# A chunk's transposed key and its scores in one bank, another order of the first LayerNorm, and shorter intervals in the scaling of token rows

## The chip, the cores and the metric

The kernel runs on one core of a Trainium2 chip. The metric is the device time of one execution in microseconds (us). The core has five engines with queues of their own, which work at once and wait for each other through semaphores: TensorE (PE in the profile, with its weight loads as PEld), VectorE (DVE), ScalarE (ACT), GpSimd (POOL) and SyncE (SP), whose queue issues most DMA transfers. PE writes its products to PSUM, eight banks of 512 float32 columns on 128 partitions; ACT and DVE read them from there.

## What is computed

One decoder block over 1,024 tokens behind 16 learned meta tokens, so 1,040 positions, each of width 1,024. The change touches three places of it: the LayerNorm that comes first, the mLSTM mixer, and the `alpha * h` that the second LayerNorm adds.

```python
h = LN(concat(meta, x))                       # the first LayerNorm
p = h @ w_in + b_in                           # -> u_s5 | q | k | v | o | i | f | g_s5 | g_m
y_s5 = GLU(GELU(S5(u_s5)))
y_m  = (o * HeadNorm(mLSTM(q, k, v, i, f))) @ m_w_out
h = LN(alpha * h + (sigmoid(g_s5) * y_s5 + sigmoid(g_m) * y_m) @ w_o)
h = LN(alpha * h + relu(h @ w_up + b_up)**2 @ w_down)
...
# mLSTM, four heads, chunk by chunk with a running state (c, n):
s = einsum("bhsd,bhjd->bhsj", q_c, k_c) * w_intra       # scores
num = s @ v_c + w_inter * (q_c @ c_st)
den = sum(s) + w_inter * (q_c . n_st)
c_new = decay * c_st + sum_j w_k[j] * outer(k_c[j], v_c[j])
```

## The kernel before

Products that need more than one pass over the array are made from a high and a low part of each factor (`whi`, `wlo`, `hT_hi`, `hT_lo`): three matmuls (L235 to L237, `mm3`) for each product. A job is a block of columns of the combined projection; it loads raw weights (`wraw`), ACT rounds them to `whi` (L221), DVE takes the rest as `wlo` (L222), and PE runs through the jobs in the order of a list. Beside the jobs there are lanes: generators (mLSTM, convolution, S5, the scaling of token rows) that yield an interval after each step. `mm3` advances a clock after every second of its terms by an estimate of the time that they take on PE, and each lane whose next step has come due by that clock issues it there (`pump`). A scheduler then settles each engine's order; only weight splits are raised in priority.

PSUM is handed out in two rings: five banks with the tag `mm` and three with the tag `sd` (`sdps`). Dependencies are kept by bank: two engines that use one bank, even other columns of it, follow one another.

**The first LayerNorm** (`ln0_pipe`, L1278 to L1447) is laid out by hand, as the list of tokens `LN0_PROG` (L66 to L76). Rows come in nine tiles `x0` to `x8` of 128 positions (the last of 16), in the groups 0, 1, 2-3, 4-5 and 6-8. The tokens are:

- `sT0 sT1` are DVE's statistics of tile T (L1291, two halves), `gT` their sum (L1296), `qG` ACT's square root for a group (L1300), `cG0` to `cG3` four small DVE steps to its inverse (L1306 to L1312), `bT` the shift that ACT needs (L1317).
- `nTa`, `nTd`, `nTl`, `nTh` normalise tile T, on ACT (L1328), on DVE (L1330), or on DVE by halves (L1326). `TT` transposes it on PE (L1343) into four banks that two tiles share, two blocks of 128 rows of width in each (`ln`), or, for the first two tiles, four blocks in each.
- `uTK`, `vPK`, `zK` copy block K out of a bank, scaled and shifted (`hf`), by ACT (L1360, suffix `a`) or DVE (L1362, suffix `d`). `HPJ` rounds half J of the pair P to `hT_hi` (ACT, L1381) and sends `hf` to DRAM, `LPJ` takes the rest as `hT_lo` (DVE, L1379).
- `WI` and `lI` split the weights of job I (L221, L222). `FIT` is job I over tile T in plain float32 (L1398). `AIB`, `BIB`, `CIB` are its three passes over block B of 256 positions (L1390: `whi` by `hT_hi`, `whi` by `hT_lo`, `wlo` by `hT_hi`), and `EIB` is ACT's copy of the sum (L298).

The order of the tokens is, but for the scheduler's shifts, the order on each engine. PE needs the four `sd` and `mm` banks of a pair emptied before it can transpose the next pair into them.

**mLSTM** (L440 to L536), for each of four heads over nine chunks, issues `A(c+1)` and then `B(c)`. `A` transposes the chunk's key (L466, tile `pk`), which ACT scales into `kw` (L468), and multiplies key by query (L471, tile `pS`), which DVE weighs into `sw` (L473). `B` makes the output `pn` from the state `C` and from `sw` (L481, L482) and the update `pu` from `kw` (L485); DVE folds it into `C` (L490), ACT and DVE read `pn` (L499 to L503). Each of the four tiles is a bank of the ring of three. Four chunks on, `N` normalises them, and PE transposes the outcome `hraw` (L523).

**The scaling of token rows** (`ah_scale`, L1454 to L1474) starts with the last job of the projection. It loads eight tiles of rows, multiplies and adds on DVE (L1471), waiting the interval `AHY` (3.6) after each of the sixteen steps, and stores them.

Of the kernel before, what the change touches and what calls it, by code (L numbers as in the profile page):

```python
# [12 lines left out]
AF = mybir.ActivationFunctionType  # L13
OP = mybir.AluOpType
P = 128
# [7 lines left out]
DK = 128  # L23
DV = 256
NCH = 9
# [29 lines left out]
Y5 = [3.2, 1.86, 2.37, 2.47]  # L55
AFT = 0
AH_START = "run7"
AHY = 3.6
UPY = 1.0
PRY = 1.07  # L60
TBY = 1.47
# [2 lines left out]
VAFT = 2  # L64
LOAD0 = "x0 x1 w0 c0 x2 w1 c1 x3 x4 w2 x5 w3 x6"
LN0_PROG = " ".join((  # L66
# [9 lines left out]
LN0_GROUPS = ((0,), (1,), (2, 3), (4, 5), (6, 7, 8))  # L76
BLK = ((0, 256), (256, 640), (640, 1040))
# [10 lines left out]
def chunk(c):  # L88
    return (0, META) if c == 0 else (META + (c - 1) * P, P)
# [32 lines left out]
def decoder_block(  # L122
# [5 lines left out]
    v_, a_, g_, t_ = nc.vector, nc.scalar, nc.gpsimd, nc.tensor  # L128
# [9 lines left out]
    def slot(name, dt=F32):  # L138
        return big.tile([P, SLOT], dt, tag="s", name=name)
# [4 lines left out]
    def sdps(name="sd"):  # L144
        return psum.tile([P, 512], F32, tag="sd", bufs=3, name=name)
# [17 lines left out]
    ident = const.tile([P, P], F32, name="ident")  # L163
# [276 lines left out]
    def mlstm(h):  # L440
        while (h, 1) not in QK:
            yield 0.5
        qT, kT, vt = QK[h, 0], QK[h, 1], VT[h]
        gB, wiB = slot("gB"), slot("wiB")
# [5 lines left out]
        for c in range(NCH):  # L450
            c0, n = chunk(c)
# [8 lines left out]
        kws, sws, Cs = {}, {}, {}  # L460

        def A(c):
            c0, n = chunk(c)
            if c < NCH - 1:
                ps = sdps("pk")
                t_.transpose(ps[:n, :DK], kT[:, c0:c0 + n], ident)  # L466
                kws[c] = mid.tile([P, DK], F32, tag="kw", bufs=2, name="kw")
                a_.activation(kws[c][:n], ps[:n, :DK], AF.Copy, scale=gB[:n, c0 + n - 1:c0 + n])  # L468
            if c > 0:
                ps = sdps("pS")  # L470
                t_.matmul(ps[:, :P], kT[:, c0:c0 + n], qT[:, c0:c0 + n], start=True, stop=True)  # L471
                sws[c] = mid.tile([P, P], F32, tag="sw", bufs=2, name="sw")
                v_.tensor_tensor(sws[c], ps[:, :P], gB[:, c0:c0 + n], op=OP.mult)  # L473

# [30 lines left out]
        def N(half, hm):  # L505
# [12 lines left out]
            for f in range(2):  # L518
# [7 lines left out]
                yield 1.2  # L526

        A(0)
        yield 1.5
        for c in range(NCH):  # L530
            if c + 1 < NCH:
                A(c + 1)
            yield ML[h]
            B(c)
            yield ML[h]
            if c == 5:  # L536
                yield from N(0, nrm[0])
# [916 lines left out]
    def ah_scale():  # L1454
# [4 lines left out]
        for t in range(9):  # L1459
# [10 lines left out]
            for i, op in enumerate((OP.mult, OP.add)):  # L1470
                v_.tensor_tensor(r[:, :D], r[:, :D], gb[i][:, :D], op=op)  # L1471
                yield AHY
            nc.sync.dma_start(ah_dr[(t - 1) * P:t * P, :], r[:, :D])
# [31 lines left out]
    for w in ORDER.split():  # L1505
        n, i = w[0], int(w[1:])
# [669 lines left out]
```

## Time and profile before

| | before |
|---|---|
| median of 3 runs | 1524.61 us (1524.44 to 1526.71) |
| the profiled execution | 1524.99 us, of which the span from the first to the last instruction is 1523.2 us |
| mean granted clock of TensorE | 0.995 |
| DVE busy | 1049.4 us, 69% of the span |
| ACT busy | 667.9 us, 44% |
| DMA, mean rate over the span | 173 GB/s |
| the scaling's 16 steps on DVE (L1471) | 638.1 to 709.8 us of the span, 1.22 us each |

The profile is of one execution. Times in its views count from the first instruction. A row of the view of time gives the start, the length of the group, the engine, the line, the operation with output and inputs, how many, and in brackets how long the engine stood idle before it and for whom. Matmuls overlap, so that two starts, not one length, give what a matmul takes on PE. In the view of stretches the columns are the stretch, its length, PE's busy time with the number of instructions, the granted clock as a share of the full one, and DMA. In the view of waits they are who waited for whom, the sum, how often, and the longest.

The first LayerNorm fills the span up to 76.6 us, where the first job for the value projection starts (L348). Head 0 of mLSTM starts at 138.9 us and the last head's last key is transposed at 521.6 us.

### The profile page before, as it was taken

Reading aid. Unit: us, or ns where it says so; the run is one execution under the profiler, and the core shown is the slowest. Engines: PE = TensorE matmul, PEld = TensorE weight load, DVE = VectorE, ACT = ScalarE, POOL = GpSimd, SP = SyncE. Lnnn points to the kernel's source line nnn. Section 1 sums busy time; section 2 is a strip of 40 time slices with the busy share of each in tenths; the row PEclk is TensorE's granted clock in tenths of the full one; section 3 lists DMA queues with packets and bytes.
Section 4 is the critical chain, followed back from the end, with each engine's and each line's share of the span. In section 5 each row is a group of like instructions: output and inputs, shape, how many; then the busy total and the mean of one; then the engine's idle time right before and its main releaser. Section 6 shows DMA issues by size and latency. Waiting matters only on the chain.

```text
span 1523.2 us, 20345 instructions
## 1 busy us (share of the span) xinstructions
PE 1498.7 (98%) x7581; PEld 1268.1 (83%) x7581; DVE 1049.4 (69%) x1901; ACT 667.9 (44%) x1033; POOL 81.8 (5%) x183
## 2 busy tenths in 40 slices
PE   7999899999999999999999999999999999999997
PEld 7998799988998888887888888888888888888886
DVE  7776755675675356788797575766666579867786
ACT  5641634454565533345443253444444524333330
POOL 0000000033330000000000001000000000000000
PEclk9999999999999999999999999999999999999999
DMA  8513332256754238876352248644443799667543
GB/s 303 192 46 91 82 98 87 70 156 155 183 136 125 69 126 331 297 264 211 111 193 69 97 128 268 187 153 149 145 147 128 251 374 343 211 236 246 196 166 111
DMA packets 123635, 264.06 MB, mean 173 GB/s; under 512 B 14648, under 2 KB 36864, under 8 KB 123536
## 3 DMA queue, kind: packets, MB, share of 16 engines
q1 hardware_dynamic: 112064, 233.79, 45.1%
q0 software_dynamic: 11472, 28.97, 7.7%
q8 instruction: 60, 0.98, 0.3%
q14 instruction: 39, 0.32, 0.1%
HBM read 191.67 MB, written 86.64 MB: 183 GB/s over the span
## 4 chain that ended last, share of the span: by engine, by line
PE 74%; issue 17%; DMA 4%; DVE 3%; ACT 1%; SPq 0%; POOLq 0%; ACTq 0%; DVEq 0%
PE mm L237 19%; PE mm L235 19%; PE mm L236 19%; PE sd L236 3%; PE sd L235 3%; PE sd L237 3%; PE mm L1390 2%; DMA wdr<-in_wdn_dram 1%; DMA x<-in_x_dram 1%; PE pn L481 1%; PE pn L482 1%; PE pu L485 1%; DMA da<-act_dr 1%; DMA wiB<-wrow_dr 1%; PE pS L471 1%
## 5 line engine op out<-in xcount | busy, mean ns | idle before, releaser
L235 PE MATMUL mm<-hT_hi,whi 128*128 128x512 f32 (+3 forms) x600 | 228.7, 381 | 1.7 <-ACT whi L1068 1.7
L237 PE MATMUL mm<-hT_hi,wlo 128*128 128x512 f32 (+3 forms) x600 | 223.9, 376 | 0.6 <-DVE wlo L1069 0.6
L236 PE MATMUL mm<-hT_lo,whi 128*128 128x512 f32 (+3 forms) x600 | 224.1, 374 | 0.0
L235 PEld LDWEIGHTS mm<-hT_hi,whi 128*128 128x128 f32 x600 | 112.9, 188 | 19.9 <-ACT whi L1068 2.2
L237 PEld LDWEIGHTS mm<-hT_hi,wlo 128*128 128x128 f32 x600 | 112.9, 188 | 19.7 <-DVE wlo L1069 1.6
L236 PEld LDWEIGHTS mm<-hT_lo,whi 128*128 128x128 f32 x600 | 113.0, 188 | 16.3
L1875 ACT ACTIVATE dwh<-wdr 128x1024 fp32r<-128x1024 f32 x56 | 58.9, 1053 | 107.0 <-DVE wdr L1860 39.2
L237 PE MATMUL sd<-dwh,dal 128*128 128x512 f32 x240 | 94.4, 393 | 0.0
L236 PE MATMUL sd<-dwl,dah 128*128 128x512 f32 x240 | 94.3, 393 | 0.0
L235 PE MATMUL sd<-dwh,dah 128*128 128x512 f32 x240 | 92.0, 393 | 0.0
L1872 DVE TENSOR_TENSOR dal<-da,dah 128x1024 fp32r<-128x1024 f32 x56 | 68.2, 1219 | 25.7 <-ACT dah L1871 9.7
L236 PE MATMUL mm<-dwl,dah 128*128 128x512 f32 (+1 forms) x224 | 84.7, 378 | 0.1
L237 PE MATMUL mm<-dwh,dal 128*128 128x512 f32 (+1 forms) x224 | 84.6, 378 | 0.0
L235 PE MATMUL mm<-dwh,dah 128*128 128x512 f32 (+1 forms) x224 | 83.3, 377 | 0.0
L1871 ACT ACTIVATE dah<-da 128x1024 fp32r<-128x1024 f32 x56 | 58.8, 1052 | 53.2 <-DMA da<-act_dr 32.3
L222 DVE TENSOR_TENSOR wlo<-wraw,whi 128x1024 fp32r<-128x1024 f32 (+1 forms) x44 | 53.6, 1221 | 34.0 <-ACT whi L221 32.9
L1876 DVE TENSOR_TENSOR dwl<-wdr,dwh 128x1024 fp32r<-128x1024 f32 x56 | 68.3, 1220 | 9.6 <-ACT dwh L1875 9.0
L235 PE MATMUL mm<-whi,hT_hi 128*128 128x256 f32 (+1 forms) x256 | 73.9, 289 | 0.0
L237 PE MATMUL mm<-whi,hT_lo 128*128 128x256 f32 (+1 forms) x256 | 72.7, 284 | 0.0
L236 PE MATMUL mm<-wlo,hT_hi 128*128 128x256 f32 (+1 forms) x256 | 72.6, 284 | 0.0
L237 PE MATMUL mm<-th,wul 128*128 128x512 f32 x156 | 61.5, 394 | 0.0
L236 PE MATMUL mm<-tl,wuh 128*128 128x512 f32 x156 | 61.4, 394 | 0.0
(481 smaller groups left out, 3669.9 us busy)
## 6 DMA issues: line engine op xcount, KB each, us to landing
da<-act_dr SPq DMA_DIRECT2D x56, 512.0 KB, 5.7
wdr<-in_wdn_dram SPq DMA_DIRECT2D x56, 512.0 KB, 6.5
wur<-in_wup_dram SPq DMA_DIRECT2D x32, 512.0 KB, 4.9
act_dr<-upy SPq DMA_DIRECT2D x64, 256.0 KB, 2.8
wraw<-in_wf_dram SPq DMA_DIRECT2D x28, 512.0 KB, 5.9
wu_dr<-wpre SPq DMA_DIRECT2D x21, 512.0 KB, 6.0
wpre<-wu_dr POOLq DMA_DIRECT2D x21, 512.0 KB, 5.4
wraw<-ws_dr SPq DMA_DIRECT2D x32, 256.0 KB, 3.5
```

Source lines behind the costliest of these rows:

```text
L222: todo.append(lambda e=v_, r=r, hi=hi, lo=lo, n=n: e.tensor_tensor(lo[:, :n], r[:, :n], f32(hi[:, :n]), op=OP.subtract))
L235: t_.matmul(ps, ah, bh, start=(i == 0 and part[0]), stop=False, skip_group_check=skip)
L236: t_.matmul(ps, ah, bl, start=False, stop=False, skip_group_check=skip)
L237: t_.matmul(ps, al, bh, start=False, stop=(i == n - 1 and part[1]), skip_group_check=skip)
L471: t_.matmul(ps[:, :P], kT[:, c0:c0 + n], qT[:, c0:c0 + n], start=True, stop=True)
L481: t_.matmul(pn[:, :257], qi[:, c0:c0 + n], Cs[c][:, :257], start=True, stop=False)
L482: t_.matmul(pn[:, :257], sws[c], vt[c][:, :257], start=False, stop=True)
L1390: t_.matmul(acc[w][:, :c1 - c0], jobs[i].w[0][a][:, k * P:(k + 1) * P], (hT_hi, hT_lo)[b][:, k, c0:c1], start=(first and k == 0), stop=(la ...
L1871: a_.activation(ah[:, :D], a[:, :D], AF.Copy)
L1872: v_.tensor_tensor(alo[:, :D], a[:, :D], f32(ah[:, :D]), op=OP.subtract)
L1875: a_.activation(wh, raw[i], AF.Copy)
L1876: v_.tensor_tensor(wl, raw[i], f32(wh), op=OP.subtract)
```

## The change

First, `A(c)` takes one bank `pkS` where it took two: the transposed key goes to columns 128 to 255, the scores to columns 0 to 127. PE does both one behind the other, then ACT reads the key, then DVE the scores. Second, `LN0_PROG` is rewritten: the copies of a bank go to one engine, where they alternated between two; the splits `W0` and `W1` stand earlier, and so do the statistics of tiles 4 and 5 and `n4d`; `L20`, `L21` and the statistics of tile 7 stand behind one another later. Third, `AHY` is 2.8 instead of 3.6.

```diff
-AHY = 3.6
+AHY = 2.8
...
-    "X30 s00 s01 g0 q0 s10 c00 c01 c02 c03 n0l n0h s11 g1 T0l T0h u00a u01a q1 u02d u03a c10 c11 c12 c13 n1d",
-    "u04a u05a u06d u07a F00 s20 s21 F10 T1 u10a u11d u12a u13d u14a u15d u16a u17d F20 g2 s30 s31 g3 W0 H00",
-    "F01 q2 H01 c20 c21 c22 c23 b2 b3 F11 n2a n3a E00 L00 L01 F21 E10 W1 s40 s41 g4 T2 l1 W2 E20 s50 s51 g5 q3",
-    "T3 l0 W3 c30 c31 c32 F30 v11a v13d v12a c33 n4d v17a v16a v10d F31 b5 H10 v14d v15d n5a l3 L10 T4 H11 s70",
-    "T5 E30 L11 A01 v26a v22a v20d B01 v21d v23d C01 v25d H20 v24d A11 v27d E01 B11 L20 H21 C11 L21 A02 E11",
-    "s71 B02 l2 C02 g7 s60 A22 E02 s61 g6 B22 s80 s81 C22 g8 q4 A31 E22 c40 c41 c42 c43 B31 b8 b7 b6 n8a C31",
-    "n7a A12 n6a B12 E31 C12 T8 E12 T7 z83a z82d z86a z84d z80a z85d z81a T6 z87a H8 L8 A32 v33a v30d v31a",
-    "v37d B32 v34a v36d v35a v32d C32 H31 A21 E32 L31 H30 B21 L30 C21 A03 E21 B03 C03 A33 E03 B33 C33 A13 E33",
+    "X30 s00 s01 g0 q0 s10 c00 c01 c02 c03 n0l n0h s11 g1 T0l T0h u00a q1 u01a u02a u03a u04d u05d c10 c11",
+    "u06d u07d c12 c13 n1d W0 F00 s20 s21 W1 F10 g2 s30 s31 T1 g3 u10a u11a u12a u13a q2 u14d u15d u16d u17d",
+    "F20 H00 c20 c21 c22 c23 b2 b3 H01 F01 n2a s40 s41 g4 n3a F11 s50 s51 g5 q3 E00 L00 F21 E10 c30 c31 c32",
+    "c33 b5 T2 n4d L01 E20 n5a T3 W2 l1 F30 v10a v11a v12a v13a v14d v15d v16d v17d F31 H10 l0 W3 H11 T4 L10",
+    "T5 E30 L11 s60 s61 A01 B01 C01 v20a v21a v22a v23a v24d v25d v26d v27d E01 H20 g6 A11 l2 B11 H21 s70 s71",
+    "C11 L20 E11 g7 A02 L21 B02 s80 s81 C02 g8 q4 E02 A22 l3 B22 c40 c41 c42 c43 C22 b8 b7 b6 E22 A31 n8a B31",
+    "n7a C31 n6a A12 E31 B12 C12 T8 E12 T7 z80d z81d z82d z83d z84d z85d z86d z87d T6 H8 L8 A32 v30a v31a v32a",
+    "v33a v34d v35d v36d v37d B32 C32 H31 H30 A21 E32 L31 B21 L30 C21 A03 E21 B03 C03 A33 E03 B33 C33 A13 E33",
...
         def A(c):
             c0, n = chunk(c)
+            ps = sdps("pkS")
             if c < NCH - 1:
-                ps = sdps("pk")
-                t_.transpose(ps[:n, :DK], kT[:, c0:c0 + n], ident)
+                t_.transpose(ps[:n, P:P + DK], kT[:, c0:c0 + n], ident)
+            if c > 0:
+                t_.matmul(ps[:, :P], kT[:, c0:c0 + n], qT[:, c0:c0 + n], start=True, stop=True)
+            if c < NCH - 1:
                 kws[c] = mid.tile([P, DK], F32, tag="kw", bufs=2, name="kw")
-                a_.activation(kws[c][:n], ps[:n, :DK], AF.Copy, scale=gB[:n, c0 + n - 1:c0 + n])
+                a_.activation(kws[c][:n], ps[:n, P:P + DK], AF.Copy, scale=gB[:n, c0 + n - 1:c0 + n])
             if c > 0:
-                ps = sdps("pS")
-                t_.matmul(ps[:, :P], kT[:, c0:c0 + n], qT[:, c0:c0 + n], start=True, stop=True)
                 sws[c] = mid.tile([P, P], F32, tag="sw", bufs=2, name="sw")
                 v_.tensor_tensor(sws[c], ps[:, :P], gB[:, c0:c0 + n], op=OP.mult)
```

Behind `A`, every line of the new program stands one lower than in the old one.

On DVE, in the first LayerNorm, the inverse root of the group of tiles 4 and 5 (`y_147`) and the normalisation of tile 4 (`n4d`, the row with `x_120`) stood in the old program behind `L00`, `L01` and the splits `l1` and `l0`, with small steps of S5 and a copy (L1362) between them:

```order
L1306 RECIPROCAL y_147<-y_147 128x2
L572 SCALAR_TENSOR_TENSOR s_t_1210<-s_t_1209,s_t_1210 128x16
L1308 SCALAR_TENSOR_TENSOR u_152<-mv_142,y_147 128x2
L573 TENSOR_SCALAR s_dt<-s_t_1210 128x16
L577 TENSOR_SCALAR s_t_1209<-s_t_1209 128x16
L1310 SCALAR_TENSOR_TENSOR u_152<-u_152,y_147 128x2
L1362 TENSOR_SCALAR hf<-ln_335,ln0t 128x256
L575 SCALAR_TENSOR_TENSOR s_dt<-s_dt,s_t_1210 128x16
L578 CAST s_ni<-s_t_1209 128x16
L1312 SCALAR_TENSOR_TENSOR y_147<-u_152,y_147 128x2
L575 SCALAR_TENSOR_TENSOR s_dt<-s_dt,s_t_1210 128x16
L1330 TENSOR_SCALAR x_120<-x_120,mv_142,y_147 128x1024
```

In the new one they stand ahead of the splits (L222) and ahead of the copies of the pair of tiles 2 and 3:

```order
L1307 RECIPROCAL y_147<-y_147 128x2
L1309 SCALAR_TENSOR_TENSOR u_152<-mv_142,y_147 128x2
L1311 SCALAR_TENSOR_TENSOR u_152<-u_152,y_147 128x2
L568 TENSOR_SCALAR s_t_1210<-s_lam 128x16
L1313 SCALAR_TENSOR_TENSOR y_147<-u_152,y_147 128x2
L569 TENSOR_SCALAR s_t_1209<-s_t_1210 128x16
L1318 SCALAR_TENSOR_TENSOR u_152<-mv_142,y_147 128x1
L1331 TENSOR_SCALAR x_120<-x_120,mv_142,y_147 128x1024
L1380 TENSOR_TENSOR hT_lo<-hf,hT_hi 128x4x256
L297 MEMSET cpre 128x3
L570 TENSOR_SCALAR s_t_1209<-s_t_1209 128x16
L222 TENSOR_TENSOR wlo<-wraw,whi 128x1024
```

So the normalisation of tile 4 has passed `L01` (the row L1380), two splits and the copy.

Further down on DVE, the low parts of the pair of tiles 4 and 5 (`L20`, `L21`) followed the copies of that pair almost at once, in the old program:

```order
L1362 TENSOR_SCALAR hf<-ln_408,ln0t 128x256 x2
L575 SCALAR_TENSOR_TENSOR s_dt<-s_dt,s_t_1210 128x16
L1362 TENSOR_SCALAR hf<-ln_409,ln0t 128x256
L1362 TENSOR_SCALAR hf<-ln_410,ln0t 128x256 x2
L1362 TENSOR_SCALAR hf<-ln_411,ln0t 128x256
L576 TENSOR_SCALAR s_dt<-s_dt 128x16
L1379 TENSOR_TENSOR hT_lo<-hf,hT_hi 128x4x256
L579 TENSOR_TENSOR s_dt<-s_dt,s_ni 128x16
L1379 TENSOR_TENSOR hT_lo<-hf,hT_hi 128x4x256
L1291 BN_STATS st_424<-x_133 128x6
L222 TENSOR_TENSOR wlo<-wraw,whi 128x1024
```

In the new one there are statistics of tiles 6 and 7 (`x_128`, `x_133`) and a split ahead of each or between them:

```order
L1292 BN_STATS st_435<-x_128 128x6 x2
L1363 TENSOR_SCALAR hf<-ln_410,ln0t 128x256 x2
L1363 TENSOR_SCALAR hf<-ln_411,ln0t 128x256 x2
L573 SCALAR_TENSOR_TENSOR s_t_1210<-s_t_1209,s_t_1210 128x16
L1297 BN_AGGR mv_143<-st_435 128x2
L222 TENSOR_TENSOR wlo<-wraw,whi 128x1024
L1292 BN_STATS st_495<-x_133 128x6 x2
L1380 TENSOR_TENSOR hT_lo<-hf,hT_hi 128x4x256
L574 TENSOR_SCALAR s_dt<-s_t_1210 128x16
L578 TENSOR_SCALAR s_t_1209<-s_t_1209 128x16
L1297 BN_AGGR mv_143<-st_495 128x2
L1380 TENSOR_TENSOR hT_lo<-hf,hT_hi 128x4x256
```

DVE has two copies fewer there (four of the pair's eight, where it had six), and two statistics and a split more ahead of `L20`.

On PE, in head 0 of mLSTM, one chunk's transposed key and scores were parted by a matmul of the job that runs beside them:

```order
L485 MATMUL pu<-v_881,kw 128x257
L466 MATMUL pk<-ident,kT 128x128
L237 MATMUL mm<-hT_hi,wlo 128x512
L471 MATMUL pS<-qT,kT 128x128
L235 MATMUL mm<-hT_hi,whi 128x512
```

In the new program they stand together:

```order
L486 MATMUL pu<-v_881,kw 128x257
L466 MATMUL pkS<-ident,kT 128x128
L468 MATMUL pkS<-qT,kT 128x128
L237 MATMUL mm<-hT_hi,wlo 128x512
L235 MATMUL mm<-hT_hi,whi 128x512
```

Of 28 such pairs, 5 stood together before and all 28 do now. From 570 us of the old span on, PE, DVE and ACT have the same instructions in the same order in both programs, and that holds for all sixteen steps of the scaling; with `AHY` changed alone, every engine keeps its order from the first to the last instruction.

## The prediction

> **What bounds the kernel now.** I read the page first, then the stretches, then who waited for whom on PE, then PE's rows in order of time where it waits.
>
> ```profile
> PE 1498.7 (98%) x7581; PEld 1268.1 (83%) x7581; DVE 1049.4 (69%) x1901; ACT 667.9 (44%) x1033; POOL 81.8 (5%) x183
> ```
>
> PE is busy for 98% of the span. What a change can win lies in the other 2%, in matmuls that run below the full clock, and in the number of matmuls, which stays.
>
> ```profile
> 0.00:100.00 100.00, 91.55 (x710) 88.02 (x711) 77.54 (x207) 55.42 (x84) 4.54 (x25) 0.97 0.57 199
> 100.00:200.00 100.00, 94.98 (x586) 84.72 (x586) 61.88 (x219) 40.92 (x64) 5.12 (x26) 0.98 0.29 83
> 200.00:300.00 100.00, 100.00 (x648) 95.03 (x647) 60.92 (x156) 43.30 (x69) 5.26 (x11) 1.00 0.31 87
> ```
>
> The first stretch holds the LayerNorm, the second head 0 of mLSTM; the granted clock (the third number from the end) lies under 1 in both. In the third, with most of heads 0 and 1 behind it or under way, PE is without a gap. The waits name the places:
>
> ```profile
> PE pt L523 <- DVE hraw L516: 3.1, 1, 3.1
> PE ln L1343 <- DVE x L1330: 3.1, 1, 3.1
> ...
> PE pS L471 <- ACT kw L468: 1.5, 3, 0.5
> ```
>
> The wait for L1330 lies where the LayerNorm's order is changed, that for `kw` where the bank is shared; the one for `hraw` is touched by neither.
>
> **The LayerNorm.** PE in order of time:
>
> ```profile
> 10.33 5.39 PE L1398 MATMUL mm<-hf,wraw 128*128 128x128 f32 x32
> 15.56 1.04 PE L1343 MATMUL ln<-ident,x 128*128 128x128 f32 x8
> 16.43 7.31 PE L1398 MATMUL mm<-hf,wraw 128*128 128x128 f32 x64
> 23.58 2.13 PE L1343 MATMUL ln<-ident,x 128*128 128x128 f32 x16
> 25.54 3.74 PE L1398 MATMUL mm<-hf,wraw 128*128 128x128 f32 x32
> 32.34 0.95 PE L1343 MATMUL ln<-ident,x 128*128 128x128 f32 x4 [3.06 <-DVE x L1330]
> 33.76 3.19 PE L1343 MATMUL ln<-ident,x 128*128 128x128 f32 x12 [0.48 <-DVE hf L1362]
> 36.60 2.06 PE L1390 MATMUL mm<-hT_hi,whi 128*128 128x256 f32 x8
> 38.46 1.65 PE L1390 MATMUL mm<-hT_lo,whi 128*128 128x256 f32 x8
> 39.95 1.10 PE L1390 MATMUL mm<-hT_hi,wlo 128*128 128x256 f32 x8
> 40.89 1.10 PE L1390 MATMUL mm<-hT_hi,whi 128*128 128x256 f32 x8
> ...
> 64.20 1.27 PE L1390 MATMUL mm<-hT_hi,whi 128*128 128x272 f32 x8 [0.80 <-ACT hT_hi L1381]
> ```
>
> *What goes.* The stall before `T4` ends when DVE has normalised tile 4:
>
> ```profile
> 31.38 0.81 DVE L1330 TENSOR_SCALAR x<-x,mv,y 128x1024 f32<-128x1024 f32 x1
> ```
>
> In the new order that step has passed two splits, `L01` (1.13 us of DVE each, rows below) and a copy (0.45). So it starts by 31.38 - 3.4 - 0.45 = 27.5 at the latest and ends at 28.3, before PE gets to `T4` (29.28, or 0.5 earlier, below); chained from the landing of tile 5 on, it starts at about 24. The 0.48 us, a wait for DVE's copies out of a bank that both engines empty by turns, goes with the turns. From the end of the x32 group (25.54 + 3.74 = 29.28) to `C01` at 39.95 PE took 10.67 us. Without a stall and at the full clock that is sixteen transposes (23.58 to 25.54: 1.96) and two passes (39.95 to 40.89: 0.94 each), 3.84 us. So **6.8 us** lie there: 3.5 in the two stalls, and 3.3 in matmuls at half the clock:
>
> ```profile
> 29.44:32.86 3.42, 0.52 (x3) 1.00 0.03 10
> 32.86:36.27 3.41, 2.80 (x12) 0.50 0.95 338
> 36.27:39.68 3.41, 3.41 (x18) 0.50 0.79 282
> ```
>
> The columns are PE's busy time, then its clock. The clock fell after a window of 3.41 us in which PE worked 0.52, and stayed low for two such windows. With no idle stretch over 1.5 us (below) it has no reason to fall.
>
> *What comes earlier at the start.* The first x32 group takes 5.23 us from start to start, where the x64 group gives 3.58 for as many (7.15 / 2); the rest is waiting for copies:
>
> ```profile
> DVE hf L1362 <- ACT hf L1360: 5.7, 7, 2.6
> ```
>
> Seven waits of DVE for ACT on copies of a bank (up to 70 us). Four copies by one engine follow each other without them, but four in a row by ACT take as long as two engines by turns would without the waits, so I take 0.5 of the 1.65 us, with bounds 0.3 and 0.9.
>
> *What is late next.* `A01` follows `T5` at 30.7 in the new order. I chain DVE and ACT forward by the starts of before:
>
> ```profile
> 33.54 1.22 DVE L222 TENSOR_TENSOR wlo<-wraw,whi 128x1024 fp32r<-128x1024 f32 x1
> ...
> 34.75 1.22 DVE L1379 TENSOR_TENSOR hT_lo<-hf,hT_hi 128x1024 fp32r<-128x1024 f32 x1
> 35.89 0.69 DVE L1291 BATCH_NORM_STATS2 st<-x 128x6 f32<-128x512 f32 x1
> ...
> 38.80 1.90 DVE L1362 TENSOR_SCALAR hf<-ln,ln0t 128x256 f32<-128x256 f32 x4
> ```
>
> A split or a low part occupies DVE for 1.13 us, half a tile's statistics for 0.6, a copy for 0.45. `L10` and `L11` end at 32.6, and the second half of `B01` waits for `L11`: 0.6 us, and 0.1 for `H11` before it. Behind `L11` DVE has two half statistics (1.2), four copies (1.8), the split `l2` (1.13), two more half statistics (1.2) and small steps (0.2) before `L20`, which therefore starts at 38.1 and ends at 39.3. PE has run `A01` to `A02` by 37.9 and waits 1.4 us at `B02`; its second half waits 1.0 more for `L21` (end 40.7). So 3.1 us of new waits, none long enough to leave a window empty. After them nothing is late that was not: the 0.8 us before `A03` waited for ACT's `H30`, behind copies by turns that are now in two uninterrupted rows, and goes.
>
> Sum: 6.8 + 0.5 + 0.8 - 3.1 = **5.0 us less**. Bounds: 3.0, if each new wait is half as long again and the start gives 0.3 (5.0 - 1.55 - 0.2, and 0.3 for small ones); 7.5, if DVE runs ahead as far as it did before and half the waits vanish (5.0 + 1.55 + 0.4, rounded up by 0.5). What follows from 76.6 us on only moves forward: its weights are loaded behind the store of `H8`, which is earlier too.
>
> **The shared bank.** In the dense stretches PE pays for a matmul of another shape. Three cases before, all among products of 256 columns, which take 0.118 us alone: a key by itself, a pair, and scores by themselves.
>
> ```profile
> 217.51 0.27 PE L466 MATMUL pk<-ident,kT 128*128 128x128 f32 x1
> 217.54 0.37 PE L235 MATMUL mm<-whi,hT_hi 128*128 128x256 f32 x1
> 217.74 0.28 PE L236 MATMUL mm<-wlo,hT_hi 128*128 128x256 f32 x1
> ...
> 219.05 0.38 PE L471 MATMUL pS<-qT,kT 128*128 128x128 f32 x2
> ...
> 219.39 0.28 PE L236 MATMUL mm<-wlo,hT_hi 128*128 128x256 f32 x1
> ...
> 230.32 0.27 PE L466 MATMUL pk<-ident,kT 128*128 128x128 f32 x1
> 230.43 0.39 PE L471 MATMUL pS<-qT,kT 128*128 128x128 f32 x2
> ...
> 230.77 0.28 PE L236 MATMUL mm<-wlo,hT_hi 128*128 128x256 f32 x1
> ```
>
> The key costs 0.23 - 0.12 = 0.11, the scores 0.34 - 0.12 = 0.22, the two together 0.45 - 0.12 = 0.33. Standing together neither saves nor costs; 23 pairs by 0.01 us of reading error bound it at 0.2 us either way.
>
> The price is on the other side: `sw` on DVE now waits until ACT has written `kw`, and what is behind it on DVE (the fold into `C`, the statistics of `pn`, the jobs' splits) waits too, and PE for these. In the dense stretches products of a job stand between the scores and the `pn` that needs `sw`, and DVE had time there, since it was `sw` that waited for PE:
>
> ```profile
> DVE sw L473 <- PE pS L471: 21.3, 12, 3.3
> ```
>
> So I cost it at nothing. If that cover were gone, each of 28 chunks would pay up to 0.5 us, what `pS` waits for now. Only in the end of head 0 (153 to 162 us) has PE nothing else: the three waits for `kw` go, but each next `pn` then needs its own old bank back from ACT's copy and DVE's statistics, which are about as late. I take 0, between 1.0 less and 1.0 more.
>
> **The scaling's interval** moves no instruction on any engine, so it brings 0. I see no resource that could be freed by a number that only sets due times which fall between the same neighbours.
>
> **The second low clock.** The 3.1 us before L523 emptied a window, too:
>
> ```profile
> 162.55:165.97 3.42, 0.32 (x3) 1.00 0.13 52
> 165.98:169.39 3.41, 3.41 (x14) 0.50 0.00 0
> ```
>
> The row at half the clock costs half of 3.41, so 1.7 us; the stall itself stays. Both emptied windows start at whole multiples of 3.413 us from one another (29.44 and 162.55: 39 of them). If that grid keeps its place against the start, the stall, 5 us earlier at 157.6 to 160.7, lies half in the window to 159.14 and half in the next. Each then holds 1.5 to 1.9 us of work, and the clock stays: 1.7 us less. The trace has no window so half filled but the one with 2.80, behind which a low clock stayed one window longer, so this is the least certain term. [...]
>
> **Sum.** 1524.99 - 5.0 + 0 + 0 - 1.7 = 1518.3 for an execution like the profiled one, which was 0.4 above the median of its three runs; so **1518.0**.
>
> **The rivals.**
>
> 1. *The clock falls all the same behind the 3.1 us.* Then 1519.7. For it: the stall stays, and where in a window it falls is open.
> 2. *The new waits eat the gain.* `L20` late by 3 us more (say because `l2` or the copies wait for ACT) makes PE idle 4.4 us at `B02`, empties a window there and brings the half clock back with 3.3 us: 1518.0 + 3.0 + 3.3 = 1524.3. Against it: the sum of DVE's work ahead of `L20` leaves no room for more than 1 us of waiting unless ACT's row of copies is late.
> 3. *Slower: `sw` behind `kw`.* With one bank PE may not write it again before both readers are done, and `sw` waits in DVE's queue behind ACT. If `pn` then waited 0.5 us in each of 28 chunks, 14 us would come on: 1532. It decides against the change from about 0.35 us a chunk on (6.7 + 3.0 over 28). Against it: the 21.3 us of DVE's waiting above, and PE's 100.00 of 100 us from 200 to 300. [...] By the rows the ring still leaves two other banks for `pn` and `pu`.
> 4. *The new order does not do what it says*: DVE still reaches `n4d` late because tile 5's statistics, now ahead of it, wait for the tile's landing. Then some 3 us of the stall stay, and with them the low clock: 1518.0 + 3.0 + 3.3, so 1524 too.
>
> **Chances.** My forecast 0.40, the first rival 0.32, the second 0.10, the third 0.08, the fourth 0.10. The range takes in the LayerNorm's bounds (2.5 down, 2.0 up), the serial stretch (1.0 either way) and all rivals but the third: 1515.0 to 1524.5. About 0.2%, 3.05 us, is what a measurement of this kernel can tell from no change; faster than 1521.6 are the first case, most of the first rival and little else: 0.70; within 3.05 us 0.22; slower 0.08.
>
> **What would show it.** Right: no row of 3 us before `T4`, clock 1.00 from 29 to 43 us, a wait of 1 to 1.5 us at `B02` and of about 0.6 at `B01`, the first value job at 71.6 instead of 76.6 us, and from 180 us on PE's rows as dense as now. Wrong: PE waiting for `sw` or `pkS` in the dense stretches, a window at 0.50 before 45 us, or a first value job later than 74 us.

## The result, and the profile after

| | before | after |
|---|---|---|
| median | 1525.63 us (1524.44 to 1526.71, 4 runs) | 1517.57 us (1516.78 to 1519.37, 4 runs) |
| ratio | | 0.9943, interval 0.9931 to 0.9955 |
| the profiled execution (its span) | 1524.99 us (1523.2) | 1516.78 us (1515.0) |

The change makes the kernel 0.57% faster. The fourth run of before came with those of after and lifts its median by 1.0 us; 1517.57 is 0.4 below the forecast.

PE's share of the page of the new kernel, and who PE waited for there:

```profile
PE 1494.0 (99%) x7581; PEld 1266.1 (84%) x7581; DVE 1048.4 (69%) x1906; ACT 666.1 (44%) x1028; POOL 81.6 (5%) x183
```

```profile
PE pt L524 <- DVE hraw L517: 3.2, 1, 3.2
PE mm L1391 <- DVE hT_lo L1380: 2.0, 3, 1.2
...
PE mm L1391 <- ACT hT_hi L1382: 0.8, 1, 0.8
PE pn L482 <- DVE C L491: 0.7, 3, 0.2
```

Lines from `A` on stand one lower than before. The 3.1 us stall before `T4` (`ln` for `x`, L1330) is gone, and so are the three waits of the scores for `kw`. New are those for `hT_lo` (`L11`, `L20`, `L21`), for `H11`, and three short ones of `pn` for `C`. The stall for `hraw` stays.

PE's rows in the LayerNorm of the new kernel, in order of time:

```profile
8.44 1.11 PE L1344 MATMUL ln<-ident,x 128*128 128x128 f32 x8 [1.70 <-DVE x L1327]
...
14.12 1.04 PE L1344 MATMUL ln<-ident,x 128*128 128x128 f32 x8
...
27.45 0.38 PE L1344 MATMUL ln<-ident,x 128*128 128x128 f32 x2
28.09 1.72 PE L1344 MATMUL ln<-ident,x 128*128 128x128 f32 x14 [0.26 <-DVE hf L1363]
...
31.03 0.74 PE L1391 MATMUL mm<-hT_hi,whi 128*128 128x256 f32 x4 [0.76 <-ACT hT_hi L1382]
...
32.48 0.74 PE L1391 MATMUL mm<-hT_lo,whi 128*128 128x256 f32 x4 [0.23 <-DVE hT_lo L1380]
33.06 1.10 PE L1391 MATMUL mm<-hT_hi,wlo 128*128 128x256 f32 x8
...
39.09 0.74 PE L1391 MATMUL mm<-hT_lo,whi 128*128 128x256 f32 x4 [1.16 <-DVE hT_lo L1380]
40.45 0.75 PE L1391 MATMUL mm<-hT_lo,whi 128*128 128x256 f32 x4 [0.62 <-DVE hT_lo L1380]
...
50.58 2.56 PE L1344 MATMUL ln<-ident,x 16*128 16x16 f32 x24
...
70.67 1.13 PE L348 MATMUL mm<-whi,meta_hl 128*48 128x264 f32 x8
```

The first row with real tiles starts at 8.44 against 9.13 us before: 0.69 us that belong to the start of the execution (the rows for tile 0 are the same). Counted from there, `T1` starts at 5.68 (before: 6.43), `T4` at 19.0 (23.2), `C01` at 24.6 (30.8) and the first value job at 62.2 (67.5).

The table splits the profiled executions at four such starts: the first transpose of a real tile, the first value job (L348), head 0's first key (L466) and the first transpose of `hraw` (L523, in the new numbering L524). The last three columns are the stretch from there to the first matmul of S5's `s5z`, the stretch from head 0's first key to the first product with `gelh` (L235, at 547.46 us before and 540.21 after), and the starts of the half-clock stretches, without the last one at the end of the kernel.

| | LayerNorm | value job to key | key to `hraw` | `hraw` to `s5z` | key to `gelh` | half clock from |
|---|---|---|---|---|---|---|
| before | 67.47 | 62.26 | 26.80 | 154.93 | 408.61 | 32.9, 166.0 |
| after | 62.23 | 62.27 | 25.44 | 154.26 | 407.27 | 158.6 |
| e1, LayerNorm alone | 62.67 | 62.27 | 27.45 | 155.38 | 409.77 | 162.4 |
| e2, bank alone | 66.51 | 62.26 | 25.39 | 153.98 | 407.17 | 33.9, 163.6 |
| e3, interval alone | 66.85 | 62.26 | 27.43 | 155.99 | 410.30 | 31.1, 164.2 |
| e4, after with a busy stall | 63.76 | 62.27 | 25.35 | 153.32 | 406.36 | 11.1, 41.9 |
| e5, after again | 64.26 | 62.29 | 25.44 | 154.26 | 407.26 | 41.7, 161.1 |
| e6, `L20` early | 59.26 | 62.07 | 25.41 | 154.09 | 407.20 | 155.9 |
| e7, e6 with a busy stall | 59.23 | 62.07 | 25.32 | 153.41 | 406.52 | none |
| e8, after with turns | 66.49 | 62.02 | 25.39 | 154.39 | 407.57 | 164.5 |
| e9, before with one engine a bank | 65.09 | 62.31 | 27.31 | 159.07 | 409.96 | 32.2, 165.4 |
| e10, after with two banks | 63.57 | 62.27 | 27.91 | 155.48 | 410.32 | 41.2, 164.0 |
| e11, e6 with later transposes | 59.56 | 62.07 | 27.93 | 151.91 | 407.41 | 11.4 |

From before to after: 0.69 at the start, 5.24 in the LayerNorm, 1.34 from key to `gelh` and 0.95 behind that make the span's 8.2 us. Of the 0.95, most lies near 690 us, where PE waits for the next weights: for `whi` 1.7 us before and 1.4 after, for `wlo` 0.6 and nothing. The wait for `wlo` is 0.5 to 0.7 us in the profiles of before, e1, e2, e7, e9 and e10 and at most 0.2 in the others. Kernels with and without each of the three parts are on both sides, so it is not shown to come from the change.

The stretch up to `s5z` can only be compared between kernels that have the same work in it. Of the products with 256 columns 350 lie in it in before, e1, e3 and e10, 360 in e9, and 343 in the kernels with the shared bank; seven of them take 0.83 us. Up to `gelh` all have the same instructions, but for the sixteen that e4 and e7 add. (e11 runs two chunks more ahead of `hraw`; key to `s5z` is 179.84 us there and 179.50 in e6.)

The end of head 0, one chunk before and one after:

```profile
155.14 0.27 PE L466 MATMUL pk<-ident,kT 128*128 128x128 f32 x1
155.93 0.49 PE L471 MATMUL pS<-qT,kT 128*128 128x128 f32 x2 [0.52 <-ACT kw L468]
156.25 0.60 PE L481 MATMUL pn<-C,qi 128*128 128x257 f32 x2
156.69 0.60 PE L482 MATMUL pn<-v,sw 128*128 128x257 f32 x2
157.12 0.60 PE L485 MATMUL pu<-v,kw 128*128 128x257 f32 x2
157.55 0.27 PE L466 MATMUL pk<-ident,kT 128*128 128x128 f32 x1
```

```profile
148.60 0.27 PE L466 MATMUL pkS<-ident,kT 128*128 128x128 f32 x1
148.71 0.39 PE L468 MATMUL pkS<-qT,kT 128*128 128x128 f32 x2
149.34 0.70 PE L482 MATMUL pn<-C,qi 128*128 128x257 f32 x2 [0.24 <-DVE C L491]
149.88 0.60 PE L483 MATMUL pn<-v,sw 128*128 128x257 f32 x2
150.31 0.60 PE L486 MATMUL pu<-v,kw 128*128 128x257 f32 x2
```

The period was 157.55 - 155.14 = 2.41 us and is 2.14 (the next key starts at 150.74). The scores no longer stand behind ACT's copy of the key; what `pn` waits for instead is the fold into `C`, half as long.

### The profile page after: what moved, and what is told of

It is laid out like the page before. It is cut to its first block, busy times and chain, and to the rows that moved or that the text cites. A ratio compares the mean times of both kernels' runs of the same rounds, so it can differ in the third digit from the quotient of the medians.

```text
span 1515.0 us, 20348 instructions
## 1 busy us (share of the span) xinstructions
PE 1494.0 (99%) x7581; PEld 1266.1 (84%) x7581; DVE 1048.4 (69%) x1906; ACT 666.1 (44%) x1028; POOL 81.6 (5%) x183
## 4 chain that ended last, share of the span: by engine, by line
PE 74%; issue 17%; DMA 5%; DVE 3%; ACT 1%; SPq 0%; POOLq 0%; DVEq 0%; ACTq 0%
PE mm L237 19%; PE mm L235 19%; PE mm L236 19%; PE sd L235 3%; PE sd L236 3%; PE sd L237 3%; DMA da<-act_dr 2%; PE mm L1391 2%; DMA x<-in_x_dram 1%; PE pn L482 1%; PE pu L486 1%; PE pn L483 1%; DMA wdr<-in_wdn_dram 1%; DMA act_dr<-upy 1%; PE pt L524 1%
## 5 line engine op out<-in xcount | busy, mean ns | idle before, releaser
L235 PE MATMUL mm<-hT_hi,whi 128*128 128x512 f32 (+3 forms) x600 | 228.6, 381 | 1.4 <-ACT whi L1069 1.4
L235 PEld LDWEIGHTS mm<-hT_hi,whi 128*128 128x128 f32 x600 | 113.0, 188 | 19.3 <-ACT whi L1069 1.8
L235 PE MATMUL sd<-dwh,dah 128*128 128x512 f32 x240 | 92.0, 393 | 0.0
L235 PE MATMUL mm<-dwh,dah 128*128 128x512 f32 (+1 forms) x224 | 83.4, 378 | 0.0
L222 DVE TENSOR_TENSOR wlo<-wraw,whi 128x1024 fp32r<-128x1024 f32 (+1 forms) x44 | 53.4, 1218 | 40.0 <-ACT whi L221 39.9
L235 PE MATMUL mm<-whi,hT_hi 128*128 128x256 f32 (+1 forms) x256 | 73.5, 287 | 0.0
```

Of the source, the lines that this page charges most:

```text
L222: todo.append(lambda e=v_, r=r, hi=hi, lo=lo, n=n: e.tensor_tensor(lo[:, :n], r[:, :n], f32(hi[:, :n]), op=OP.subtract))
L235: t_.matmul(ps, ah, bh, start=(i == 0 and part[0]), stop=False, skip_group_check=skip)
```

## The experiments

All ratios are to the kernel before, run beside them.

**e1, the LayerNorm alone:** `LN0_PROG` of the new kernel in the old one.

> Only the new order of the first LayerNorm; the chunk's key and scores keep two banks, the scaling its 3.6. Theory A (the parts add): the first value job starts at about 70.7 instead of 76.6 us, the chunk period at the end of head 0 stays 2.41 us with three waits for kw, PE's start-to-start elsewhere as before; the time falls by 5.2 to 6.0 us for that (ratio 0.9961 to 0.9966). The stall of 3.1 us before the transposes of hraw then lies about 5.9 us earlier, astride two windows of 3.41 us if the grid of windows keeps its place (theory W), so that no row at half the clock follows it and another 1.7 us go (ratio about 0.995). Rival (chance): a half-clock row follows it in spite of that. Rival B (the gain is not in the LayerNorm's waits but hangs on the shared bank as well): less than 4 us.

1521.18 us, ratio 0.9977 (0.9965 to 0.9989), a smaller gain than the 0.9961 to 0.9966 expected. The LayerNorm's stretch is 62.67 us, and the chunks still take 2.41. So in the trace the parts stand side by side. In the times that is not shown: e1, e2 and e3 together have 0.23% + 0.12% + 0.00%, the whole change 0.57%, and the intervals only just overlap. And a half-clock row followed the stall, though it lay over two windows of 3.41 us:

```profile
155.59:159.00 3.41, 1.79 (x8) 1.00 0.44 154
159.01:162.42 3.41, 1.58 (x11) 1.00 0.00 0
162.42:165.83 3.41, 3.25 (x11) 0.50 0.02 5
```

The columns after the stretch are its length, PE's busy time and the clock. Behind the window with 1.79 us of work the clock stayed at 1.00, behind the next, with 1.58, it was 0.50. What theory W expected of such a stall, that the clock stays, did not come.

**e2, the bank alone:** the new `A`, with the old `LN0_PROG` and 3.6.

> Only the shared bank for a chunk's key and scores. Theory A: the chunk period at the end of head 0 falls from 2.41 to about 2.14 us, the 3.1 us stall comes 1.3 to 1.5 us earlier, the dense stretches keep their length; 1.4 us less (ratio 0.9991). Theory W: shifted by 1.4 us the stall lies astride two windows, no half-clock row follows it, and 1.7 us more go: 3.1 us less (ratio 0.998). Rival (sw behind kw blocks DVE): PE waits for sw or pkS in the dense stretches, ratio above 1.

1523.73 us, ratio 0.9988 (0.9979 to 0.9997). From key to `hraw` it takes 25.39 us, 1.41 less than before and 2.04 less than in e3, which differs from before in no instruction's place: the bank is worth 1.4 to 2.0 us there, and 1.4 to 3.1 us from key to `gelh` (the larger figure against e3, whose profile has a half-clock row more there). The rival, waits for `sw` in the dense stretches, did not come: from 170 to 560 us no wait of PE is listed before, after or in e2, so the shared bank made PE wait nowhere that it had other products between. The stall was again followed by half a clock, against theory W.

**e3, the interval alone:**

```diff
-AHY = 3.6
+AHY = 2.8
```

> Only the interval of the scaling, 2.8 for 3.6. All engines have the instructions of before in the order of before, so every theory of mine expects no change: ratio 1.000 within 0.1%. If the 0.85 us that the new kernel gained at 680 to 700 us came from the interval, the time falls by about that (0.9994) with a shorter wait for whi at 690 us.

1525.50 us, ratio 1.0000 (0.9992 to 1.0009). Nothing, as the order said. Its trace gave something else: the same order, and yet the grid of clock windows lay elsewhere (first boundary at 7.18 instead of 5.55 us), behind a window with 1.19 us of work the clock was 0.50, and behind a half-clock window with 2.17 it stayed low for one more:

```profile
27.66:31.07 3.41, 1.19 (x11) 1.00 0.55 220
31.07:34.48 3.41, 2.17 (x8) 0.50 0.54 205
```

**e4, the stall made busy:** the new kernel, and in `N`

```diff
-                ps = sdps("pt")
+                ps = sdps("pt"); [t_.transpose(ps[:, 0:P], ident, ident) for _ in range(16 if h + half + f == 0 else 0)]
```

> The new kernel with 16 transposes of the identity put in front of the first transposes of hraw, into the same bank, which real transposes overwrite afterwards. They run in the 3.2 us stall, some 1.8 us of work. Theory W: the window that held 0.3 us of work now holds about 2, the clock stays full, the stall ends when it did, and the time falls by 1.7 us against the new kernel (about 1515.9, ratio 0.9932). Rival (the low clock hangs on something else than the work in a window): a half-clock row as before, time as the new kernel's, or up to 0.1 us longer.

1518.22 us, ratio 0.9956 (0.9943 to 0.9968): against the new kernel's 0.9943 nothing can be told from the time, and the 0.9932 expected did not come. The trace can tell. The windows around the stall and two further up:

```profile
38.45:41.86 3.41, 1.74 (x12) 1.00 0.02 6
41.87:45.28 3.41, 3.41 (x18) 0.50 0.00 0
157.92:161.33 3.41, 2.06 (x19) 1.00 0.03 8
161.33:164.74 3.41, 3.01 (x17) 1.00 0.00 0
```

With 2.06 us of work in the window of the stall the clock stayed, and from `hraw` to `s5z` it takes 153.32 instead of 154.26 us: 0.9, half of what I priced. But in this execution the grid put the two waits at `B02` (39 to 40 us in the new kernel) into one window, and a third place at 7.7 us, and each cost a half-clock stretch: the LayerNorm took 63.76 instead of 62.23.

**e5, the new kernel again.**

> The new kernel unchanged, beside the three that follow, and for a second look at where its windows fall. In the six profiles so far the grid of clock windows lay differently against the first instruction each time (first boundary at 5.55, 5.02, 5.41, 6.60, 7.18 and 4.32 us), so I now expect chance to set how many half-clock windows one execution has: the stretch from the first transpose of hraw to the first s5z is 154.3 us with one such window and about 153.4 without; ratio 0.994 to 0.9955.

1518.63 us, ratio 0.9947 (0.9934 to 0.9961). The profiled execution met what e4 had met:

```profile
38.25:41.66 3.41, 1.63 (x12) 1.00 0.08 24
41.66:45.07 3.41, 3.41 (x19) 0.50 0.00 0
```

The waits at `B02`, 1.78 us together, thus went with another 1.3 to 2.0 us where the clock was 0.50 behind them (63.57 in e10 and 64.26 here against 62.23). The prediction had called them too short for that.

**e6, `L20` and `L21` early:**

```diff
-... T3 W2 l1 F30 ... F31 H10 l0 W3 H11 T4 L10",
-"T5 E30 L11 s60 s61 A01 B01 C01 v20a ... v27d E01 H20 g6 A11 l2 B11 H21 s70 s71",
-"C11 L20 E11 g7 A02 L21 B02 s80 s81 C02 ...
+... T3 W2 l0 F30 ... F31 H10 H11 W3 T4 L10",
+"T5 E30 L11 l1 A01 B01 C01 v20a ... v27d H20 E01 A11 H21 L20 B11 L21 l2 C11 s60 s61 g6",
+"E11 A02 s70 s71 g7 B02 s80 s81 C02 ...
```

> The new kernel with L20 and L21 straight behind the copies of their pair, H20 ahead of E01, l2 and the statistics of tiles 6 to 8 behind them, and l0 and l1 exchanged with H11 ahead of W3. Theory A: the waits of 1.16 and 0.62 us at B02 go, those at A01 and B01 (0.76 and 0.23) fall to 0.4 together; from the first real transpose to the first value job 62.23 becomes 59.9 us, ratio to before 0.9922 to 0.994. Rival: the root of the last group (q4) comes later and T8 to T6 wait for it, so that less than 1 us is won.

1517.05 us, ratio 0.9931 (0.9918 to 0.9944); beside it e5 had 1518.63, and each of its five runs was slower than each of these five. The LayerNorm takes 59.26 us, 2.97 less than after, and of PE's waits for `hT_lo` and `hT_hi` one of 0.3 us is left.

The rival, a late root of the last group, did not show: no row of PE waits for tiles 6 to 8.

**e7, e6 with e4's busy stall.**

> The same with the 16 transposes of the identity in the stall before hraw's. By the windows, no half-clock window can follow the stall, whatever the grid (at least half of each window is worked): from the first transpose of hraw to the first s5z 153.3 us; 0.5 to 0.9 us less than e6 on the mean. Rival: no difference to e6 in that stretch.

1514.68 us (1514.38 to 1515.25), ratio 0.9921 (0.9908 to 0.9935), the fastest of all. Its profile has no half-clock stretch but the one at the end:

```profile
152.23:155.64 3.41, 2.06 (x19) 1.00 0.16 62
155.64:159.05 3.41, 3.01 (x19) 1.00 0.00 0
```

From `hraw` to `s5z` it is 153.41 against 154.09 in e6, so 0.7. The medians differ by 2.4 us, more than that; the intervals overlap, so the larger figure is not shown. That a window worked by half cannot lower the clock was my estimate and does not hold: in e4 the clock was 0.50 behind a window with 1.74 of 3.41 us of work.

**e8, the turns back:** the new places, with the copies of each bank by both engines in the old order.

```diff
-u00a q1 u01a u02a u03a u04d u05d ... v10a v11a v12a v13a v14d v15d v16d v17d
+u00a q1 u01a u02d u03a u04a u05a ... v11a v13d v12a v17a v16a v10d v14d v15d
...
-z80d z81d z82d z83d z84d z85d z86d z87d ... v30a v31a v32a
+z83a z82d z86a z84d z80a z85d z81a z87a ... v33a v30d v31a
```

> The new kernel, but each bank is again copied out by ACT and DVE in turns, with the order and engines of before for each group of copies, at the new places. Theory A: the copies by one engine bring 0.5 us before T1, 0.2 to 0.5 before T5 and 0.8 before A03, so from the first real transpose to the first value job it takes 63.7 to 64.5 instead of 62.2 us. Rival 1: the whole gain of the LayerNorm comes from the place of n4d, and the turns cost nothing: 62.2. Rival 2: the turns make L01 and n4d late and the 3 us stall returns: over 66.

1525.23 us, ratio 0.9985 (0.9977 to 0.9994). That is 6.6 us more than e5, the new kernel beside it. The LayerNorm takes 66.49 us, without a half-clock row in it: 4.26 more than after, and only 0.4 to 1.0 less than before and e3. (The profiled execution, 1522.99 us, was the fastest of its eleven.) PE's rows:

```profile
15.43 1.04 PE L1344 MATMUL ln<-ident,x 128*128 128x128 f32 x8
...
29.92 0.66 PE L1344 MATMUL ln<-ident,x 128*128 128x128 f32 x4 [0.99 <-DVE hf L1363]
30.92 1.50 PE L1344 MATMUL ln<-ident,x 128*128 128x128 f32 x12 [0.34 <-DVE hf L1363]
...
42.51 0.74 PE L1391 MATMUL mm<-hT_lo,whi 128*128 128x256 f32 x4 [1.76 <-DVE hT_lo L1380]
43.71 0.74 PE L1391 MATMUL mm<-hT_lo,whi 128*128 128x256 f32 x4 [0.47 <-DVE hT_lo L1380]
```

`T4` no longer waits for tile 4 but for the copies (`hf`) out of the banks that it needs, and the later `L20` and `L21` cost 2.2 us. The two engines wait for each other's copies again:

```profile
ACT hf L1361 <- DVE hf L1363: 4.9, 9, 0.9
...
DVE hf L1363 <- ACT hf L1361: 2.7, 4, 1.0
```

Before these two waits were 3.9 and 5.7 us; after and e9 have neither. Rival 1 falls, and so does the size in theory A. Rival 2 has the time right, over 66, but not the reason: the 3 us stall for tile 4 did not return.

**e9, one engine a bank, at the old places:** the kernel before, with the copies of each bank in e8's diff the other way round.

> The kernel before, with only the copies of each LayerNorm bank given to one engine, four blocks in a row (blocks 0 to 3 to ACT, 4 to 7 to DVE, the last tile's to DVE) at the old places. e8 put the turns' price in the new order at 4.3 us. Theory A: 0.7 to 1.0 us less before T1 and 1.3 less between T8 and the first value job, while the 3 us stall before T4 stays with n4d and hides the rest: first real transpose to first value job 64.7 to 65.5 us (before: 66.5 to 67.5), ratio 0.998 to 0.999. Rival: all 4.3 us come here too (62.5 to 63), so the new places of the other steps bring nothing.

1524.41 us, ratio 0.9985 (0.9976 to 0.9994); the LayerNorm 65.09 us, 1.8 to 2.4 less than in e3 and before. The stall before `T4` is there, in three pieces:

```profile
30.65 0.63 PE L1343 MATMUL ln<-ident,x 128*128 128x128 f32 x4 [1.52 <-DVE x L1330]
31.56 0.63 PE L1343 MATMUL ln<-ident,x 128*128 128x128 f32 x4 [0.28 <-DVE u L1317]
33.06 1.97 PE L1343 MATMUL ln<-ident,x 128*128 128x128 f32 x8 [0.88 <-ACT x L1328]
```

So in these profiles one engine a bank brings about 2 us by itself, the new places 0.4 to 1.0, and both together 4.6 to 5.2 (62.23 against 66.85 and 67.47; with a half-clock row from `B02` on, as in e5, it is down to 64.26). The medians agree that the two need each other: one engine a bank is worth 1.7 us at the old places (1524.41 against 1526.12) and 6.6 at the new ones (e5 against e8). Each alone leaves PE waiting at the same `T4`, for the other's reason.

**e10, two banks, both matmuls issued first:**

```diff
-            ps = sdps("pkS")
...
-                t_.transpose(ps[:n, P:P + DK], kT[:, c0:c0 + n], ident)
+                pk = sdps("pk")
+                t_.transpose(pk[:n, :DK], kT[:, c0:c0 + n], ident)
             if c > 0:
+                ps = sdps("pS")
                 t_.matmul(ps[:, :P], kT[:, c0:c0 + n], qT[:, c0:c0 + n], start=True, stop=True)
...
```

> The new kernel with two banks for key and scores again, but both matmuls issued ahead of kw and sw as in the new A. Theory A (the bank makes the difference): the scheduler parts them again, scores wait for kw as before, from the first key to the last pu before the stall 23.3 to 24.0 us instead of 21.87, and the time is that of e1 (ratio 0.9965 to 0.998). Rival (the order of the calls makes it): 21.9 us there.

1522.04 us, ratio 0.9974 (0.9966 to 0.9983). From key to `hraw` it takes 27.91 us, 2.47 more than after (1.4 to 2.1 were expected), with the waits of before (`PE pS L469 <- ACT kw L472`, three times 0.5). So it is the bank and not the order of the calls. Why the scores in a bank of their own wait for `kw`, by which of the three banks each tile got, I did not settle.

**e11, the transposes of `hraw` two chunks later:** e6 and, for head 0,

```diff
-            if c == 5:
-                yield from N(0, nrm[0])
+            if c == 5 and h == 0:
+                g = N(0, nrm[0])
+                yield next(g)
+                yield next(g)
+            if c == (7 if h == 0 else 5):
+                yield from (g if h == 0 else N(0, nrm[0]))
```

> The order of e6, and head 0's transposes of hraw (L524) are issued two chunks later, behind chunk 7, with the normalisation of hraw still begun behind chunk 5. Theory: PE works on chunks 6 and 7 while DVE and ACT normalise, so the 3.2 us stall before L524 shrinks to under 1 us and with it the chance of a half-clock window: 2.0 to 3.5 us less than e6, ratio 0.990 to 0.992. Rival: PE then waits as long for DVE in chunks 6 and 7, whose steps stand behind the normalisation on DVE, and less than 1 us is won.

1516.15 us, ratio 0.9935 (0.9922 to 0.9947), so no gain on e6 that the intervals show. The waits of PE in it:

```profile
PE pn L482 <- DVE C L491: 1.6, 5, 0.6
...
PE mm L235 <- ACT whi L221: 1.4, 1, 1.4
PE pu L486 <- DVE hst L503: 0.7, 1, 0.7
...
PE pt L524 <- DVE hraw L517: 0.2, 1, 0.2
```

The stall of 3.2 us is gone, and 1.6 + 1.4 + 0.7 stand in its place (0.7 of `C` were there): DVE normalises `hraw` ahead of the steps of chunks 6 and 7, and PE then waits for the next job's `whi`, which ACT splits at 161 us, behind the copies of the transposes. The rival was right: no half-clock row follows, and yet key to `gelh` takes 407.41 us against 407.20 in e6. With the transposes out of the way, the chain of chunks and the next weights hold PE up as long.

## Why the prediction was right, and where it was not

The time was foreseen within 0.5 us, and the LayerNorm's 5.0 us came out as 5.24. But two of four terms were wrong and offset each other, and luck helped a second time: the forecast was 6.6 us below the 1524.61 of three runs, the measured change is 8.1 from 1525.63, so 1.5 larger, and the later sets of before have medians of 1525.80 to 1526.92.

1. *The stall before `T4` goes, 6.8 us with its half clock.* Right: `C01` comes 6.2 us earlier, counted from the first real transpose, where the steps gave 6.8 + 0.5 - 0.7 = 6.6.
2. *0.5 us at the start.* It was 0.75, within the bounds of 0.3 and 0.9.
3. *New waits of 3.1 us.* 0.76 and 0.23 at `A01` and `B01` (forecast 0.1 and 0.6), 1.16 and 0.62 at `B02` (1.4 and 1.0): 2.8 in all. The second pair came from chaining DVE's durations. That these waits are harmless for the clock was wrong (e4, e5).
4. *0.8 before `A03`.* From `T8` to the first value job it is 20.09 us, where it was 21.42: 1.3.
5. *What is owed to what.* The forecast gave nearly all to the places of the steps, and 1.8 us to the copies by one engine. In e8 and e9 the places alone bring 0.4 to 1.0, the copies alone about 2, and only both together free `T4`. The sum was right because the change does both; the split was not.
6. *The shared bank at nothing.* For the dense stretches right: the new trace has 16 places where a key and its two score matmuls stand between products of a job, and in the median they cost 0.33 us, as forecast. For the end of head 0 the step "each next `pn` then needs its own old bank back ... about as late" failed: the wait that took the place of 0.52 us is 0.24, and it is for `C`. 1.36 us came there, outside the 1.0 that was allowed. Over the whole way from key to `gelh` the profiles with the shared bank and one half-clock row lie at 407.17 to 407.57 us (after, e2, e5, e6, e8), those with two banks at 408.61 to 410.32 (before, e1, e3, e9, e10; in e3 two such rows). Between before and after nothing is left behind `hraw`: from there to `gelh` it is 381.81 and 381.83 us.
7. *The interval at nothing.* Right (e3).
8. *The second low clock gone, 1.7 us.* Wrong, and this is the step that failed outright. It went by two conditions, that the grid keeps its place against the start and that 1.5 us of work in a window are enough. The grid did not keep its place: in the new kernel's profile the whole stall fell into one window, with 0.23 us of work, and the first boundary lay at 5.02 us there, at 5.55 before and between 4.3 and 7.2 us in the profiles of e1 to e4. And behind windows with 1.58 (e1), 1.63 (e5) and 1.74 us (e4) of work the clock was 0.50 too, so that 1.5 us are enough is not shown. All ten profiles in which PE stood still for 3.1 or 3.2 us before `hraw` have a half-clock stretch behind it, wherever the grid lay; the first rival, with chance 0.32, is what happened. The term's price was too high as well: 0.7 to 0.9 us (e4, e7) instead of 1.7. Part of the difference is that at the full clock PE waits there for others, in e7 0.19 us for `sw` and 0.21 for `whi`; the rest I cannot account for. The prediction also says that the trace of before has no window so half filled. It has one, and the clock stayed:

```profile
688.22:691.63 3.41, 1.70 (x8) 1.00 0.84 233
691.63:695.04 3.41, 3.41 (x16) 1.00 0.94 333
```

So -5.0 and -1.7 were forecast. Between the two profiles -5.2 came from the LayerNorm and -1.3 from the shared bank, which had stood at nothing; the second low clock brought none. The other 0.7 at the start and 0.95 behind `gelh` are not shown to be the change's.

## What to carry to other kernels

When two engines emptied one bank by turns, hand-overs became waits (4.9 and 2.7 us of them in e8, none after); give a bank to one engine, and give the other the next bank. A stall with two causes answers to neither edit alone: measure each with the other in place, or the sum will be put down to the wrong one. Where a matmul chain has one idle place of about 3 us, as `T4` and `hraw` here (3.1 us each before, with the clock at 0.50 behind both), ask what it does to the clock behind it, and add up two shorter waits that lie close together (those at `B02`, 1.78 us in the new kernel; in e5 the clock was 0.50 from 41.66 us on). Before comparing stretches of two traces, see that both have the same instructions in them: a border that seven products crossed looked like a gain of 0.7 us here.

## What the runs showed of the hardware

- In the profile of before the clock changed at 32.86, 39.69, 165.98 and 169.39 us, 2, 37 and 1 times 3.413 us apart, in that of after at 158.62 and 162.03. This grid of windows lay elsewhere against the start from profile to profile: the first boundary stood between 4.3 and 7.5 us in the thirteen profiles. One program met different half-clock stretches: the new kernel's LayerNorm took 62.23 us in one profile, without such a stretch, and 64.26 in another, with one. The profiles have none to two stretches per execution, besides the one at the end of the kernel; those of before and after are 3.41 or 6.83 us long. before ranged from 1522.84 to 1528.58 in 23 runs beside e1 to e4; how much of that is the grid is not shown.
- Behind windows at the full clock with 0.52 and 0.32 (before), 0.23 (after) and 1.19 us (e3) of work in 3.41 the clock was 0.50, but the busy time of the profile gives no sharp border. It was 0.50 also behind windows with 1.58 (e1), 1.63 (e5) and 1.74 us (e4), and behind 1.78 and 1.84 (e10, from 37.74 and 160.62 us) and 1.92 (e4, from 7.73 us). It stayed at 1.00 behind 1.45 (before, from 5.55 us), 1.58 (e8), 1.70 (before, from 688.22 us), 1.71 (e10), 1.79 (e1), 2.05 (after, from 680.86 us) and 2.06 (e4, e7). So between 1.45 and 1.92 us of 3.41 both happened, with busy times that are modelled.
- In four profiles the stall before `hraw` fell over two windows almost evenly. In all four the clock stayed behind the first and was 0.50 behind the second: 1.79 and 1.58 us of work in e1, 1.58 and 1.62 in e8, 1.79 and 1.71 in e9, 1.71 and 1.84 in e10. In two of them the second had more work than the first, so something besides this sum decides; what, stays open. The rows of e8:

```profile
157.66:161.07 3.41, 1.58 (x7) 1.00 0.46 154
161.07:164.48 3.41, 1.62 (x12) 1.00 0.00 0
164.49:167.90 3.41, 3.41 (x11) 0.50 0.02 5
```

- Behind a half-clock window with 2.17 us of work (e3) or 2.80 (before) the clock stayed low for one more; behind one with 3.25 (e1) it rose.
- With sixteen transposes of the identity in the 3.2 us stall the windows there held 2.06 and 3.01 us of work and the clock stayed at 1.00 (e4, e7); without them it was 0.50 behind a window with 0.23 (after).
